# Conv mixer's LayerNorm in an encoder trunk: most statistics and flips ahead of the last tap group, smaller pieces after it, three weight subtractions on GpSimd

## The chip, the core and the metric

One of the eight cores of a Trainium2 chip runs the whole program; nothing is shared with the others. The metric is the device time of one execution in microseconds (us), lower is better; the median of three runs is given. A core has five engines with a queue each, and an engine takes its instructions strictly in the order in which they stand: TensorE (PE in the profile, PEld for its weight loads), VectorE (DVE), ScalarE (ACT), GpSimd (POOL) and SyncE (SP, which here only issues DMAs). They wait for each other on semaphores. Matmuls write to PSUM, in banks of 128 x 512 floats; all other tiles lie in SBUF.

## The reference, cut to what matters

The program computes four layers on 256 tokens of width 1024. Each layer has a token mixer (retention, convolution, attention, retention) and a SwiGLU FFN. Only the mixer of layer 1, the convolution, is touched:

```python
def _conv_mixer(h, w_in, b_in, w_dw, b_dw, ln_g, ln_b, w_out, b_out):
    a = h @ w_in + b_in
    u = a[..., :D_MODEL] * jax.nn.sigmoid(a[..., D_MODEL:])
    u = lax.conv_general_dilated(
        u, w_dw[:, None, :].astype(u.dtype), window_strides=(1,), padding=[(CONV_PAD, CONV_PAD)],
        dimension_numbers=('NWC', 'WIO', 'NWC'), feature_group_count=D_MODEL) + b_dw
    u = jax.nn.silu(_layernorm(u, ln_g, ln_b))
    return u @ w_out + b_out
...
x = x + _rmsnorm(m, norm_w[i, 1])
f = _swiglu(_rmsnorm(x, norm_w[i, 2]), ffn_w_in[i], ffn_w_out[i])
```

The depthwise convolution has 31 taps. The LayerNorm runs over all 1024 channels of a token, so its mean and variance need every channel of the convolution.

## The kernel before, in words

Matrix products keep nearly full float precision by splitting each operand x into a high part h, rounded to the type fp32r, and a low part l = x - h, and adding three matmuls (h h, h l, l h). `split` (L49) does this: ScalarE casts (L50), VectorE subtracts (L51). `load_w` (L62) loads 128 x 1024 weights by a DMA of SP into the tile `raw` (seven buffers) and splits them into `wh` and `wl`. The 256 tokens are two halves of 128, t = 0 and t = 1.

The convolution splits the channels. Channels 0 to 511 are done on VectorE with channels on the partitions (`taps`, L573): for each of four blocks `cb` one multiply and 30 multiply-adds `cv = upad * w + cv` (L577), then ScalarE adds the bias into `cvp` (L585). Channels 512 to 1023 are done on TensorE (`windows`, L592) with tokens on the partitions: each of two PSUM banks `pc` begins with two matmuls that put the bias in (L597) and gets four groups `q` of 16 matmuls (L604), 128 columns a group, 64 channels of both token halves.

The LayerNorm then needs tokens on the partitions. For each t, TensorE flips (transposes) the four blocks of `cvp` into the bank `bs` (L636); VectorE takes the statistics of 256 columns at a time, two from `bs` (L639) and two from the `pc` banks (L641), and joins them (L642); GpSimd makes 1/sqrt(variance + eps) as `rs` (`rsqrt_mean`, L112 and L113); VectorE computes -mean * rs (L644) and normalises the half from `bs` (L646, 512 columns), ScalarE the half from `pc` (L648, twice 256). The result `yc` is flipped back (L662), four blocks into one bank, and each block goes through `silu` with gain and bias on ScalarE (L665) into `sy`. A split of 512 columns at a time makes `yh`, `yl`, the stationary operands of the output projection (`out_block`, L200), 48 matmuls of 512 columns for each t.

The order of instructions on an engine isn't the text's alone: a scheduler at build time orders ready instructions by priority and its own idea of durations, and that order is fixed in the program. `tc.issue_after(i)` keeps an engine's instructions of the block behind `i` on that engine's queue. Here the three first tiles of `conv_w_out` (`CONV_EARLY`) have their split behind the last tap (`last_tap`), and the other five and the first FFN weights behind the split of t = 0's second half (`CONV_FENCE`, L677). After the projection, `finish` adds the residual, normalises, and the FFN starts with `flush(0)` (flips at L162) and matmuls at L183.

Of the kernel before, what the change touches and what calls it, by code (L numbers as in the profile page):

```python
# [8 lines left out]
F32 = mybir.dt.float32  # L9
F32R = mybir.dt.float32r  # L10
# [27 lines left out]
def tile_trunk(ctx: ExitStack, tc: tile.TileContext, a):  # L38
# [7 lines left out]
    def bank(tag):  # L46
        return ps.tile([P, 512], F32, tag=tag, name=tag, bufs=4 if tag == "acc" else 2)

    def split(h, l, src):  # L49
        ia = nc.scalar.copy(h, src)  # L50
        iv = nc.vector.tensor_sub(l, src, h.bitcast(F32))  # L51
        return ia, iv
# [9 lines left out]
    def load_w(src, cols=1024, pool=None, bufs=None):  # L62
# [8 lines left out]
        cast[0], cast[1] = split(h[:, :cols], l[:, :cols], raw[:, :cols])  # L71
        return h, l
# [441 lines left out]
    def conv(j, finish, pool, prefetch):  # L514
# [76 lines left out]

        def windows(bk):  # L592

            pc = bank("acc")
            sl = slice(bk * 512, bk * 512 + 512)
            for i, row in enumerate((brh, brl)):
                nc.tensor.matmul(pc, lhsT=ones.bitcast(F32R), rhs=row[:, sl], start=(i == 0), stop=False)  # L597
            for q in range(4):
                for hf in range(2):
                    tz = wp.tile([P, 1024], F32, tag="raw", name="raw", bufs=RAWBUFS)  # L600
                    nc.sync.dma_start(tz, a["conv_tz"][j, 4 * bk + q, hf])
                    for i in range(8):
# [6 lines left out]
                            stop=(q == 3 and d == SHIFTS - 1),  # L609
                        )  # L610
            return pc
# [11 lines left out]
        pcs = [windows(bk) for bk in range((KB - VB) // 2)]  # L623

        with tc.issue_after(last_tap["v"].ins):
            wo = [load_w(a["conv_w_out"][j, k]) for k in range(CONV_EARLY)]
# [4 lines left out]
        for t in range(2):  # L631
            bs = bank("mm")
            bn = work.tile([P, 4, 6], F32, tag="bn", name="bn", bufs=2)
            ms = work.tile([P, 8], F32, tag="lnm", name="lnm", bufs=2)
            for k in range(VB):
                nc.tensor.transpose(bs[:, k * P : (k + 1) * P], cvp[:, k, t * P : (t + 1) * P], ident)  # L636
            parts = [pc.rearrange("p (g t c) -> p g t c", t=2, c=64)[:, :, t, :] for pc in pcs]
            for hh in range(2):
                nc.vector.bn_stats(bn[:, hh, :], bs[:, hh * 256 : hh * 256 + 256])  # L639
            for hh in range(2):  # L640
                nc.vector.bn_stats(bn[:, 2 + hh, :], parts[hh])  # L641
            nc.vector.bn_aggr(ms[:, 0:2], bn)  # L642
# [3 lines left out]
            nc.vector.tensor_scalar(yc[:, 0:512], bs, ms[:, 0:1], rs, op0=ALU.subtract, op1=ALU.mult)  # L646
            for hh in range(2):
                nc.scalar.activation(  # L648
                    yc[:, 512 + 256 * hh : 768 + 256 * hh].rearrange("p (g c) -> p g c", c=64),
                    parts[hh],  # L650
                    AF.Identity,
                    scale=rs,
                    bias=ms[:, 2:3],
                )
            h = const.tile([P, KB, P], F32R, tag=f"xTh{t}", name=f"yh{t}")
            l = const.tile([P, KB, P], F32R, tag=f"xTl{t}", name=f"yl{t}")
            for hh in range(2):
# [5 lines left out]
                for k in range(4):  # L663
# [8 lines left out]
                ends = split(  # L672
                    h[:, 4 * hh : 4 * hh + 4, :].rearrange("p k t -> p (k t)"),
                    l[:, 4 * hh : 4 * hh + 4, :].rearrange("p k t -> p (k t)"),
                    sy.rearrange("p k t -> p (k t)"),
                )
# [348 lines left out]
```

## Time and profile before

| what | value |
|---|---|
| median of 3 runs (lowest to highest) | 1592.09 us (1591.9 to 1592.46) |
| the profiled execution | 1592.03 us, of which its span is 1590.3 us |
| DVE, ACT, POOL busy (share of the span) | 65%, 52%, 5% |
| first matmul of `windows` (L597) | 450.9 us |
| first matmul of the FFN after the convolution (L183) | 517.31 us |

Times in the profile run from the start of the span. A row of a timeline gives start, duration, engine, line, operation, tiles (out<-in) and the number of merged instructions; in square brackets stands how long the engine had been idle and what it had waited for. The table of windows gives for each stretch its length, then for each engine the busy time and count, then the TensorE clock that was granted (1.00 is full) and the DMA share.

### The profile page before, as it was taken

What the parts mean: (1) busy time and instruction counts of PE and PEld (TensorE: products, weight loads), DVE (VectorE), ACT (ScalarE), POOL (GpSimd) and SP (SyncE); (2) the same over time, 40 slices, a digit from 0 to 9 for tenths busy, and PEclk for the clock granted to TensorE, in tenths of its full rate; (3) what the DMA queues carried; (4) which work ended last, traced back from release to release, by engine and by line L of the source; (5) the groups of instructions that cost most, each with busy time, mean ns of one, the idle gap of its engine ahead of it and who ended that gap; (6) DMA issues with size and microseconds to landing.
All of it is one profiled execution on the core that took longest, in us unless ns stands there. A gap on an engine that the chain in (4) does not pass through costs nothing.

```text
span 1590.3 us, 21093 instructions
## 1 busy us (share of the span) xinstructions
PE 1565.7 (98%) x7792; PEld 1332.6 (84%) x7792; DVE 1036.6 (65%) x1575; ACT 834.2 (52%) x1291; POOL 83.3 (5%) x123
## 2 busy tenths in 40 slices
PE   9999999999998999999999999999999999999998
PEld 6888878888896888889999999788888888878886
DVE  7756685556698755558778777755468655675452
ACT  6544464445517644446666666644456444654441
POOL 1000010001111100010000000100011000100000
PEclk9999999999998999999999999999999999999999
DMA  8646466565456754534444444745555544475530
GB/s 312 230 141 198 138 232 213 171 209 175 154 164 230 262 201 159 189 126 151 152 149 150 130 136 159 262 167 206 186 185 176 183 164 134 157 238 201 183 119 27
DMA packets 82700, 283.19 MB, mean 178 GB/s; under 512 B 9890, under 2 KB 10146, under 8 KB 82596
## 3 DMA queue, kind: packets, MB, share of 16 engines
q1 hardware_dynamic: 82084, 281.32, 52.7%
q8 instruction: 61, 1.00, 0.2%
q0 software_dynamic: 512, 0.53, 0.1%
q14 instruction: 43, 0.35, 0.1%
HBM read 280.23 MB, written 1.05 MB: 177 GB/s over the span
## 4 chain that ended last, share of the span: by engine, by line
PE 87%; DVE 5%; ACT 3%; DMA 3%; issue 2%; POOL 0%; SPq 0%; DVEq 0%; POOLq 0%; ACTq 0%
PE mm L183 57%; PE acc L200 20%; DVE cv L577 2%; PE acc L804 1%; PE aux L459 1%; DMA raw<-in_ffn_w_out 1%; PE aux L324 1%; DVE wl L51 1%; ACT wh L50 1%; PE aux L789 1%; PE acc L763 1%; DMA raw<-in_ret_w_in 1%; PE acc L761 1%; PE aux L300 1%; PE aux L728 1%
## 5 line engine op out<-in xcount | busy, mean ns | idle before, releaser
L183 PE MATMUL mm<-wh,xTh 128*128 128x512 f32 (+1 forms) x1536 | 591.1, 385 | 1.1 <-ACT xTh L50 1.1
L183 PE MATMUL mm<-wl,xTh 128*128 128x512 f32 (+1 forms) x1536 | 579.7, 378 | 0.0
L183 PE MATMUL mm<-wh,xTl 128*128 128x512 f32 (+1 forms) x1536 | 579.2, 377 | 0.0
L51 DVE TENSOR_TENSOR wl<-raw,wh 128x1024 fp32r<-128x1024 f32 (+1 forms) x432 | 497.9, 1163 | 118.2 <-ACT wh L50 104.0
L50 ACT CAST wh<-raw 128x1024 fp32r<-128x1024 f32 (+1 forms) x432 | 429.8, 1004 | 159.6 <-PE mm L183 105.3
L183 PEld LDWEIGHTS mm<-wh,xTl 128*128 128x128 f32 x1536 | 288.7, 188 | 45.9 <-DVE xTl L51 0.3
L183 PEld LDWEIGHTS mm<-wh,xTh 128*128 128x128 f32 x1536 | 289.1, 188 | 43.5 <-ACT xTh L50 1.5
L183 PEld LDWEIGHTS mm<-wl,xTh 128*128 128x128 f32 x1536 | 289.5, 188 | 41.7 <-DVE wl L51 0.5
L448 ACT ACTIVATE fsg<-mm,rsx 128x256 f32<-128x256 f32 x88 | 41.7, 474 | 168.6 <-PE mm L183 168.5
L450 DVE SCALAR_TENSOR_TENSOR fsg<-mm,rsx,fsg 128x256 f32<-128x256 f32 x88 | 42.3, 481 | 124.8 <-ACT fsg L448 124.6
L51 DVE TENSOR_TENSOR pooll<-raw,poolh 128x1024 fp32r<-128x1024 f32 x88 | 107.2, 1222 | 6.9 <-ACT poolh L50 6.2
L200 PE MATMUL acc<-poolh,fhh 128*128 128x512 f32 x344 | 107.6, 393 | 0.5 <-ACT fhh L50 0.5
L200 PE MATMUL acc<-poolh,fhl 128*128 128x512 f32 x344 | 107.2, 392 | 0.0
L200 PE MATMUL acc<-pooll,fhh 128*128 128x512 f32 x344 | 106.1, 389 | 0.0
L50 ACT CAST poolh<-raw 128x1024 fp32r<-128x1024 f32 x88 | 92.7, 1054 | 23.4 <-PE acc L200 14.6
L51 DVE TENSOR_TENSOR fhl<-aux,fhh 128x256 fp32r<-128x256 f32 x88 | 37.0, 421 | 97.9 <-ACT fhh L50 97.9
L50 ACT CAST fhh<-aux 128x256 fp32r<-128x256 f32 x88 | 32.5, 369 | 116.3 <-PE aux L459 116.3
L200 PEld LDWEIGHTS acc<-poolh,fhh 128*128 128x128 f32 x344 | 63.7, 188 | 15.1 <-ACT fhh L50 2.7
L200 PEld LDWEIGHTS acc<-pooll,fhh 128*128 128x128 f32 x344 | 64.6, 188 | 13.5
L200 PEld LDWEIGHTS acc<-poolh,fhl 128*128 128x128 f32 x344 | 64.3, 188 | 13.5
L110 POOL TENSOR_SCALAR rs<-ss 128x1 f32<-128x1 f32 x16 | 7.2, 448 | 1034.3 <-ACT junk L118 1034.2
L577 DVE SCALAR_TENSOR_TENSOR cv<-upad,wdw,cv 128x256 f32<-128x256 f32 x120 | 49.0, 478 | 0.1
(186 smaller groups left out, 1573.9 us busy)
## 6 DMA issues: line engine op xcount, KB each, us to landing
raw<-in_ffn_w_in SPq DMA_DIRECT2D x176, 512.0 KB, 4.8
raw<-in_ret_w_in SPq DMA_DIRECT2D x96, 512.0 KB, 4.9
raw<-in_ffn_w_out SPq DMA_DIRECT2D x88, 512.0 KB, 4.6
raw<-in_attn_w_in SPq DMA_DIRECT2D x96, 384.0 KB, 3.6
raw<-in_ret_w_out SPq DMA_DIRECT2D x32, 512.0 KB, 4.4
raw<-in_conv_w_in SPq DMA_DIRECT2D x16, 512.0 KB, 5.0
raw<-in_conv_tz SPq DMA_DIRECT2D x16, 512.0 KB, 4.6
gain<-in_norm_w SPq DMA_DIRECT2D x15, 512.0 KB, 5.8
```

The source lines that it names most:

```text
L50: ia = nc.scalar.copy(h, src)
L51: iv = nc.vector.tensor_sub(l, src, h.bitcast(F32))
L183: nc.tensor.matmul(out, lhsT=st[t][:, k, :], rhs=mv[:, sl], start=(n == 0), stop=(n == 23))
L200: nc.tensor.matmul(acc[hh], lhsT=st, rhs=mv[:, hh * 512 : hh * 512 + 512], start=(first and i == 0), stop=(last and i == 2),)
L300: nc.tensor.matmul(b[:, m * 256 : (m + 1) * 256], lhsT=kt[:, 2 + half, m * P : (m + 1) * P], rhs=qt[:, half, :], start=(n == 0), stop=(n = ...
L324: nc.tensor.matmul(b, lhsT=pt[:, m, t * P : (t + 1) * P], rhs=vt[:, m, :], start=(n == 0), stop=(n == 5))
L448: nc.scalar.activation(sg, b[:, 0:256], AF.Silu, scale=rsx[t])
L450: nc.vector.scalar_tensor_tensor(out=sm, in0=b[:, 256:512], scalar=rsx[t], in1=sg, op0=ALU.mult, op1=ALU.mult)
L459: nc.tensor.transpose(tp[:, k * P : (k + 1) * P], sm[:, k * P : (k + 1) * P], ident)
L577: last_tap["v"] = nc.vector.scalar_tensor_tensor(out=cv, in0=upad[:, cb, w : w + 256], scalar=wdw[:, cb, w : w + 1], in1=cv, op0=ALU.mult, ...
L728: nc.tensor.transpose(tp[:, k * P : (k + 1) * P], rf[:, k * P : (k + 1) * P], ident)
L761: nc.tensor.matmul(b[:, 0:256], lhsT=x[:, 0, ts_(t)], rhs=y[:, h, :], start=(n == 0), stop=(n == 2))
```

## The change

Four things are edited, all for the end of the convolution's mixer.

1. `windows` is cut. Bank 0 is as before. In bank 1 the bias is put into the first three groups; behind group 2 stand the calls `early(0)` and `early(1)`, then the bias of the last 128 columns and group 3, the last tap group. `early(t)` flips blocks 0 to 2 of `cvp` into `bs[t]` and takes three statistics: bank 0 (256 columns), the three flipped blocks (384), and the first three groups of bank 1 (192).
2. Behind the last tap group remain for each t one flip (block 3), statistics of 128 and of 64 columns, and the joining of now five parts.
3. The normalisation is done in four quarters of 256 columns, by VectorE and ScalarE in turn, and the split behind the silu in pieces of two blocks (256 columns) instead of four.
4. The low parts of the three early tiles of `conv_w_out` are subtracted on GpSimd instead of VectorE (`sub=nc.gpsimd`).

```diff
-    def split(h, l, src):
+    def split(h, l, src, sub=None):
         ia = nc.scalar.copy(h, src)
-        iv = nc.vector.tensor_sub(l, src, h.bitcast(F32))
+        iv = (sub or nc.vector).tensor_sub(l, src, h.bitcast(F32))
         return ia, iv
...
+        def part(bk, t, lo, hi):
+            return pcs[bk].rearrange("p (g t c) -> p g t c", t=2, c=64)[:, lo:hi, t, :]
+
+        def early(t):
+            bs[t] = bank("mm")
+            for k in range(VB - 1):
+                nc.tensor.transpose(bs[t][:, k * P : (k + 1) * P], cvp[:, k, t * P : (t + 1) * P], ident)
+            nc.vector.bn_stats(bn[t][:, 0, :], part(0, t, 0, 4))
+            nc.vector.bn_stats(bn[t][:, 1, :], bs[t][:, 0 : 3 * P])
+            nc.vector.bn_stats(bn[t][:, 2, :], part(1, t, 0, 3))
...
+            cut = 3 if bk else 4
...
+            bias(0, cut)
             for q in range(4):
+                if q == cut:
+                    early(0)
+                    early(1)
+                    bias(cut, 4)
                 for hf in range(2):
...
-            wo = [load_w(a["conv_w_out"][j, k]) for k in range(CONV_EARLY)]
+            wo = [load_w(a["conv_w_out"][j, k], sub=nc.gpsimd) for k in range(CONV_EARLY)]
...
+            nc.tensor.transpose(bs[t][:, 3 * P : 4 * P], cvp[:, 3, t * P : (t + 1) * P], ident)
+            ms = work.tile([P, 16], F32, tag="lnm", name="lnm", bufs=2)
+            nc.vector.bn_stats(bn[t][:, 3, :], bs[t][:, 3 * P : 4 * P])
+            nc.vector.bn_stats(bn[t][:, 4, :], part(1, t, 3, 4))
+            nc.vector.bn_aggr(ms[:, 0:2], bn[t][:, 0:5, :])
             rs = rsqrt_mean(ms[:, 1:2], None, LN_EPS, scale=1.0)
...
-            nc.vector.tensor_scalar(yc[:, 0:512], bs, ms[:, 0:1], rs, op0=ALU.subtract, op1=ALU.mult)
...
+            quarter = (bs[t][:, 0:256], bs[t][:, 256:512], part(0, t, 0, 4), part(1, t, 0, 4))
+            for q4, src in enumerate(quarter):
+                dst = yc[:, 256 * q4 : 256 * q4 + 256]
...
+                if q4 % 2 == 0:
+                    nc.vector.tensor_scalar(dst, src, ms[:, 0:1], rs, op0=ALU.subtract, op1=ALU.mult)
+                else:
+                    nc.scalar.activation(dst, src, AF.Identity, scale=rs, bias=ms[:, 2:3])
...
-                ends = split(
-                    h[:, 4 * hh : 4 * hh + 4, :].rearrange("p k t -> p (k t)"),
...
+                    if k % 2:
+                        ends = split(
+                            h[:, cb - 1 : cb + 1, :].rearrange("p k t -> p (k t)"),
```

What the scheduler makes of it is seen in the order of the built programs. First TensorE's queue before, at the end of bank 1's last two pieces (L604 are the tap matmuls, L636 the flips of `cvp`, L662 the first flip of the normalised `yc`):

```order
L604 MATMUL acc<-raw,uw 128x128 [waits DMAHW2_49,DMASW7_49]
L604 MATMUL acc<-raw,uw 128x128 x7
L604 MATMUL acc<-raw,uw 128x128 [waits DMAHW3_49]
L604 MATMUL acc<-raw,uw 128x128 x7
L636 MATMUL mm<-ident,cvp 128x128 [waits Activation_49] x4
L636 MATMUL mm<-ident,cvp 128x128 x4
L662 MATMUL aux<-ident,yc 128x128 [waits DVE_49]
```

The same place of TensorE's queue now (L601 are the flips of `early`, L663 the two flips of block 3, L615 the bias, L634 the tap matmuls, L687 the flip of `yc`):

```order
L601 MATMUL mm<-ident,cvp 128x128 [waits Activation_49] x3
L601 MATMUL mm<-ident,cvp 128x128 x3
L663 MATMUL mm<-ident,cvp 128x128 [waits Activation_49]
L663 MATMUL mm<-ident,cvp 128x128 [waits DVE_49]
L615 MATMUL acc<-cbrh,ones 128x128 [waits DVE_49]
L615 MATMUL acc<-cbrl,ones 128x128
L634 MATMUL acc<-raw,uw 128x128 [waits DMAHW2_49,DMASW7_49]
L634 MATMUL acc<-raw,uw 128x128 x7
L634 MATMUL acc<-raw,uw 128x128 [waits DMAHW3_49]
L634 MATMUL acc<-raw,uw 128x128 x7
L687 MATMUL aux<-ident,yc 128x128 [waits DVE_49]
```

All eight flips, those of block 3 too, now stand ahead of the last tap group. The first L663 waits for ScalarE's `cvp` of block 3, made from the last tap; the second for VectorE's L603 of t = 1; and the bias L615 for VectorE's L604 of t = 1, which reads the same PSUM bank.

VectorE's queue before, from the last taps to the normalisation of t = 0 (L641 and L639 are statistics of `pc` and of `bs`):

```order
L577 SCALAR_TENSOR_TENSOR cv<-upad,wdw,cv 128x256 [waits DVE_49] x54
L641 BN_STATS bn<-acc 128x6 [waits PE_49]
L577 SCALAR_TENSOR_TENSOR cv<-upad,wdw,cv 128x256 [waits DVE_49] x3
L51 TENSOR_TENSOR wl<-raw,wh 128x1024 [waits DMAHW4_49,Activation_49]
L51 TENSOR_TENSOR wl<-raw,wh 128x1024 [waits DMAHW5_49,Activation_49]
L51 TENSOR_TENSOR wl<-raw,wh 128x1024 [waits DMAHW6_49,Activation_49]
L639 BN_STATS bn<-mm 128x6 [waits PE_49]
L639 BN_STATS bn<-mm 128x6
L641 BN_STATS bn<-acc 128x6
L639 BN_STATS bn<-mm 128x6 [waits PE_49]
L642 BN_AGGR lnm<-bn 128x2 [waits DVE_49]
```

VectorE's queue now at that place (L602, L603 and L604 are the statistics of `early`, first of t = 0, then of t = 1; L665 those of block 3, L666 those of the last tap group):

```order
L577 SCALAR_TENSOR_TENSOR cv<-upad,wdw,cv 128x256 [waits DVE_49] x54
L602 BN_STATS bn<-acc 128x6 [waits PE_49]
L577 SCALAR_TENSOR_TENSOR cv<-upad,wdw,cv 128x256 [waits DVE_49]
L603 BN_STATS bn<-mm 128x6 [waits PE_49]
L577 SCALAR_TENSOR_TENSOR cv<-upad,wdw,cv 128x256 [waits DVE_49]
L604 BN_STATS bn<-acc 128x6
L577 SCALAR_TENSOR_TENSOR cv<-upad,wdw,cv 128x256 [waits DVE_49]
L602 BN_STATS bn<-acc 128x6
L603 BN_STATS bn<-mm 128x6 [waits PE_49]
L604 BN_STATS bn<-acc 128x6
L665 BN_STATS bn<-mm 128x6 [waits PE_49] x2
L666 BN_STATS bn<-acc 128x6 [waits PE_49]
```

The three subtractions are gone from it, two more statistics stand between the last three taps, and those of t = 1 right behind them.

GpSimd's queue now, from the last of the DMAs that fill `uw` on (before, the three L51 rows weren't there, and nothing else differs):

```order
L566 DMA uw<-su 64x128 [waits DMASW7_49]
L51 TENSOR_TENSOR wl<-raw,wh 128x1024 [waits DMAHW4_49,PE_49,Activation_49]
L51 TENSOR_TENSOR wl<-raw,wh 128x1024 [waits DMAHW5_49,PE_49,Activation_49]
L51 TENSOR_TENSOR wl<-raw,wh 128x1024 [waits DMAHW6_49,PE_49,Activation_49]
L112 TENSOR_SCALAR rs<-lnm 128x1 [waits DVE_49]
L113 TENSOR_TENSOR rs<-rs,nhalf 128x1 [waits Pool_49]
```

The subtractions come ahead of the `rs` of both token halves. SP's queue has the same loads in the same order; three loads of `conv_w_out` that waited for VectorE's or TensorE's release of a `raw` buffer now wait for GpSimd's.

More of the change, by code (lines that the diff above doesn't have):

```diff
@@ L60, in tile_trunk, with load_w @@
     cast = [None, None]
[L62 removed]
+    def load_w(src, cols=1024, pool=None, bufs=None, sub=None):
         raw = wp.tile([P, 1024], F32, tag="raw", name="raw", bufs=RAWBUFS)
@@ L70, in load_w @@
             l = pool.tile([P, 1024], F32R, tag="pooll", name="pooll", bufs=bufs)
-        cast[0], cast[1] = split(h[:, :cols], l[:, :cols], raw[:, :cols])
+        cast[0], cast[1] = split(h[:, :cols], l[:, :cols], raw[:, :cols], sub)
         return h, l
@@ L590, in taps, with bias @@
             )
+        bs = [None, None]
+        bn = [work.tile([P, 8, 6], F32, tag="bn", name="bn", bufs=2) for t in range(2)]
+        def part(bk, t, lo, hi):
[7 more added lines that the diff above has]
+            nc.vector.bn_stats(bn[t][:, 2, :], part(1, t, 0, 3))
         def windows(bk):
             pc = bank("acc")
-            sl = slice(bk * 512, bk * 512 + 512)
-            for i, row in enumerate((brh, brl)):
-                nc.tensor.matmul(pc, lhsT=ones.bitcast(F32R), rhs=row[:, sl], start=(i == 0), stop=False)
+            pcs.append(pc)
+            cut = 3 if bk else 4
+            def bias(lo, hi):
+                for i, row in enumerate((brh, brl)):
+                    nc.tensor.matmul(
+                        pc[:, lo * P : hi * P],
+                        lhsT=ones.bitcast(F32R),
+                        rhs=row[:, bk * 512 + lo * P : bk * 512 + hi * P],
+                        start=(i == 0),
+                        stop=False,
+                    )
+            bias(0, cut)
             for q in range(4):
+                if q == cut:
+                    early(0)
+                    early(1)
+                    bias(cut, 4)
                 for hf in range(2):
@@ L608, in windows @@
                             start=False,
-                            stop=(q == 3 and d == SHIFTS - 1),
+                            stop=(q in (3, cut - 1) and d == SHIFTS - 1),
                         )
-            return pc
         wc = {}
@@ L622, in conv @@
             taps(cb)
-        pcs = [windows(bk) for bk in range((KB - VB) // 2)]
+        pcs = []
+        for bk in range(2):
+            windows(bk)
         with tc.issue_after(last_tap["v"].ins):
-            wo = [load_w(a["conv_w_out"][j, k]) for k in range(CONV_EARLY)]
+            wo = [load_w(a["conv_w_out"][j, k], sub=nc.gpsimd) for k in range(CONV_EARLY)]
         yh, yl = {}, {}
@@ L631, in conv @@
         for t in range(2):
[L632 to L642, printed above, removed]
+            nc.tensor.transpose(bs[t][:, 3 * P : 4 * P], cvp[:, 3, t * P : (t + 1) * P], ident)
[3 more added lines that the diff above has]
+            nc.vector.bn_aggr(ms[:, 0:2], bn[t][:, 0:5, :])
             rs = rsqrt_mean(ms[:, 1:2], None, LN_EPS, scale=1.0)
```

16 lines of the change are left out of this document (5 added, 11 removed).

## The prediction

> **What bounds the kernel now.** I read the page first, then the windows and waits around the end of the convolution, then the timelines of single engines there.
>
> ```profile
> span 1590.3 us, 21093 instructions
> PE 1565.7 (98%) x7792; PEld 1332.6 (84%) x7792; DVE 1036.6 (65%) x1575; ACT 834.2 (52%) x1291; POOL 83.3 (5%) x123
> PE 87%; DVE 5%; ACT 3%; DMA 3%; issue 2%; POOL 0%; SPq 0%; DVEq 0%; POOLq 0%; ACTq 0%
> ```
>
> TensorE sets the time; what is to be won are stretches where it waits or runs at a lower clock. The waits of TensorE between 474 and 520 us, and the windows (length, busy time and count of PE, PEld, DVE, ACT, POOL, then the granted clock, DMA share, GB/s):
>
> ```profile
> PE aux L662 <- DVE yc L646: 4.3, 1, 4.3
> PE aux L662 <- ACT sy L665: 1.2, 1, 1.2
> PE acc L200 <- DVE yl L51: 0.3, 1, 0.3
> 478.03:484.55 6.52, 4.51 (x41) 4.27 (x39) 6.45 (x12) 3.56 (x6) 0.00 (x0) 1.00 0.88 278
> 484.55:494.79 10.24, 6.82 (x23) 5.57 (x24) 6.41 (x14) 7.84 (x16) 1.49 (x4) 0.50 0.46 180
> ```
>
> The largest wait of this stage is 4.3 us for the normalised `yc`, and the clock is 0.50 for 10.24 us from 484.55 on. The timeline of TensorE, then of VectorE and ScalarE, shows what the wait consists of:
>
> ```profile
> 467.11 14.56 PE L604 MATMUL acc<-raw,uw 128*128 128x128 f32 x128
> ...
> 481.51 1.04 PE L636 MATMUL mm<-ident,cvp 128*128 128x128 f32 x8
> 486.81 1.97 PE L662 MATMUL aux<-ident,yc 128*128 128x128 f32 x8 [4.27 <-DVE yc L646]
> 489.94 1.09 PE L662 MATMUL aux<-ident,yc 128*128 128x128 f32 x4 [1.16 <-ACT sy L665]
> 490.68 1.20 PE L200 MATMUL acc<-wh,yh 128*128 128x512 f32 x2
> ```
>
> ```profile
> 475.74 2.45 DVE L577 SCALAR_TENSOR_TENSOR cv<-upad,wdw,cv 128x256 f32<-128x256 f32 x6
> 478.11 0.42 DVE L641 BATCH_NORM_STATS2 bn<-acc 128x6 f32<-128x256 f32 x1
> 478.45 1.50 DVE L577 SCALAR_TENSOR_TENSOR cv<-upad,wdw,cv 128x256 f32<-128x256 f32 x3
> 479.87 3.49 DVE L51 TENSOR_TENSOR wl<-raw,wh 128x1024 fp32r<-128x1024 f32 x3
> 483.28 0.75 DVE L639 BATCH_NORM_STATS2 bn<-mm 128x6 f32<-128x256 f32 x2
> 483.95 0.41 DVE L641 BATCH_NORM_STATS2 bn<-acc 128x6 f32<-128x256 f32 x1
> 484.28 0.41 DVE L639 BATCH_NORM_STATS2 bn<-mm 128x6 f32<-128x256 f32 x1
> 484.61 0.24 DVE L642 BATCH_NORM_AGGREGATE lnm<-bn 128x2 f32<-128x24 f32 x1
> 484.78 0.37 DVE L639 BATCH_NORM_STATS2 bn<-mm 128x6 f32<-128x256 f32 x1
> ...
> 485.95 0.80 DVE L646 TENSOR_SCALAR yc<-mm,lnm,rs 128x512 f32<-128x512 f32 x1
> ```
>
> ```profile
> 475.47 1.05 ACT L50 CAST wh<-raw 128x1024 fp32r<-128x1024 f32 x1 [19.27 <-DMA raw<-in_conv_w_out]
> ...
> 478.05 0.52 ACT L585 ACTIVATE cvp<-cv,chv 128x256 f32<-128x256 f32 x1
> 478.99 1.04 ACT L50 CAST wh<-raw 128x1024 fp32r<-128x1024 f32 x1 [0.42 <-DMA raw<-in_conv_w_out]
> 479.99 0.54 ACT L585 ACTIVATE cvp<-cv,chv 128x256 f32<-128x256 f32 x1
> ```
>
> The last tap group ends at 481.67 (467.11 + 14.56), the last tap at 479.95. Then VectorE does three subtractions (3.49 us) before its statistics, and TensorE waits. The change removes the 3.49 us from this chain. But before, the last tap group ran from 478.03 to 481.67 (a quarter of 14.56 is 3.64) beside the last taps; now, as the rows of TensorE's queue show, it stands behind flips and a bias that wait for the last tap and for statistics behind it. So the time of the last tap decides, and the three subtractions now run on GpSimd beside those taps.
>
> **The price of the subtractions on GpSimd.** No row shows one. The nearest rows (line, engine, operation, then busy time and mean ns of one; or start and duration):
>
> ```profile
> L532 POOL MEMSET uw<- 128x1152 f32 x1 | 1.1, 1063 | 5.3 <-PE acc L190 5.3
> L110 POOL TENSOR_SCALAR rsx<-ss 128x1 f32<-128x1 f32 x16 | 21.6, 1348 | 57.7 <-ACT junk L118 44.6 <-DVE xg L141 13.0
> 484.96 0.19 POOL L112 TENSOR_SCALAR rs<-lnm 128x1 f32<-128x1 f32 x1 [29.09 <-DVE lnm L642]
> 207.20 2.13 POOL L110 TENSOR_SCALAR rsx<-ss 128x1 f32<-128x1 f32 x1 [4.25 <-ACT junk L118]
> 206.81 2.35 DVE L51 TENSOR_TENSOR wl<-raw,wh 128x1024 fp32r<-128x1024 f32 x2
> 1399.76 0.82 POOL L110 TENSOR_SCALAR rsx<-ss 128x1 f32<-128x1 f32 x1 [2.46 <-ACT junk L118]
> 1399.80 1.29 DVE L141 TENSOR_TENSOR xg<-x,gain 128x512 f32<-128x512 f32 x2
> ```
>
> A memset writes 1152 columns in 1.063 us, so 1024 take 0.94: the lower end, one pass. Two inputs and an output one after the other are three passes, 2.83: the upper end. I take two passes, 1.9 us (two inputs in turn, the output beside).
>
> The other rows show a collision. A one-column operation of GpSimd takes 0.19 us while VectorE works from PSUM (484.96, beside the statistic at 484.78), but 2.13 us when it starts under two `wl` subtractions of VectorE, which read two SBUF tiles: it ends at 209.33, right behind them (209.16). The one at 1399.76 ended at 1400.58, half a us before the second of two `xg` products did (1401.09). So GpSimd is shut out while VectorE reads two SBUF tiles, and gets in after one or two of its instructions. A tap (`upad`, `cv`) is of that kind; a statistic from PSUM isn't. No row shows the reverse, a tap held up by a long GpSimd instruction, since none is long. Lower end: taps aren't held. Upper end: a tap waits for the whole subtraction. I take the upper end, since the row at 207.20 is such a full exclusion, seen from the other side.
>
> [...]
>
> **The sum.** It is made against the profiled execution, 1592.03 us (span 1590.3 and 1.73 around it), which is the median, 1592.09, to 0.06.
>
> 1. *Last tap.* Two statistics of 256 columns are 0.335 apart each (483.28 to 483.95), so the added ones, 384 and 192 columns, cost 0.50 and 0.25: 479.95 becomes 480.7. The first cast ends at 476.52, so GpSimd gets in at about 477.3, after one or two more taps of 0.4 us; the second and third follow with a tap or two between, all before the last tap (the third cast is late by then, behind the held `cvp` of block 2, and ends at about 481.2, before GpSimd asks for it). 3 x 1.9 = 5.7, of which some 0.6 hides under the PSUM statistics: **485.8**.
> 2. *Last tap group.* Statistics of t = 1 behind the tap, 0.34 + 0.50 + 0.25 = 1.1: the bias starts at 486.95 (`cvp` of block 3 and its two flips are done by then). Bias and group are 0.25 + 3.64 at full clock. TensorE will have been idle from 478.03 on but for eight flips (1.04), longer than the 4.27 that came with the clock of 0.50; there, half clock lasted 4.1 us into steady work (490.68 to 494.79). So 4.1 us do 2.05, 1.84 remain: end at **492.9** instead of 481.67.
> 3. *Group to `yc`.* Only 64 columns remain: 0.3 with the handshakes, then as before 484.61 to 485.95, 1.34: `yc` starts at 494.55, not 485.95. What remains of GpSimd's queue is long done.
> 4. *`yc` to the projection.* Before 485.95 to 490.68, 4.73. The pieces:
>
> ```profile
> 486.13 1.02 ACT L648 ACTIVATE yc<-acc,lnm,rs 128x256 f32<-128x256 f32 x2 [4.09 <-DVE lnm L644]
> 487.97 1.85 ACT L665 ACTIVATE sy<-aux,chv 128x128 f32<-128x128 f32 x5 [0.81 <-PE aux L662]
> 489.69 0.64 ACT L50 CAST yh<-sy 128x512 fp32r<-128x512 f32 x1
> ```
>
> ScalarE's pair starts 0.18 behind and takes 1.02; two flips 0.4; in ScalarE's queue three silus of 0.35 stand ahead of the first cast, half as wide, 0.4: 3.05, with a handshake 3.1. Gain 1.6. The projection starts at 494.55 + 3.1 = **497.65**, 7.0 later than 490.68.
> 5. *Behind it.* The idle stretch before the projection is again long, so half clock costs t = 0 what it did: 0. ScalarE's casts of the other five `conv_w_out` tiles start 3.0 instead of 1.5 after the projection's start (five silus, four pieces); they were needed with spare time:
>
> ```profile
> 492.19 6.78 ACT L50 CAST wh<-raw 128x1024 fp32r<-128x1024 f32 x7
> 493.32 5.77 DVE L51 TENSOR_TENSOR wl<-raw,wh 128x1024 fp32r<-128x1024 f32 x5 [0.25 <-ACT wh L50]
> 497.50 0.62 PE L200 MATMUL acc<-wl,yh 128*128 128x512 f32 x2
> ```
>
> The first `wl` of these is done at 494.55 and used at 497.50: of 2.95 spare, 1.4 remain. Without that cover it would cost up to 1.5. The loads that now wait for GpSimd's release of `raw` land well before these casts. For t = 1 the 0.3 wait for `yl` goes, and the queue has the flips of the next stage later; I count -0.5. From there on TensorE is full as before, so nothing is made good.
>
> Total: 7.0 - 0.5 = **+6.5 us, 1598.5**. With one pass for a subtraction (0.94) the three cost 2.9 less: +3.6; with three passes +9.3.
>
> **Rivals.**
>
> *The taps aren't held up (or GpSimd gives way).* The last tap ends at 480.9 (0.2 for the first flips, which need `cvp` of block 2 at 478.57), the bias starts at 482.0, the group ends at 485.9 at full clock or some 487.2 at half, `yc` starts 1.65 later, the projection 3.1 after that: 490.65 or 491.95, that is 0 or +1.3; with -0.5, **1591.5 to 1592.8**. For it: no row shows a held tap. If GpSimd comes only behind the taps, it ends at 480.9 + 5.7 = 486.6, about when `rs` is needed; at 2.83 us each `rs` would be 2.5 late, 1595.
>
> *Not slower: the clock doesn't fall at all.* The place is TensorE between 478.03 and the projection. If taps aren't held and the eight flips split the idle stretches so that the clock stays at 1.00, the group ends at 485.9, the projection starts as before, and it also saves what half clock cost from 490.68 to 494.79, half of 4.1: -2.05 - 0.5, **1589.5**. It decides when no idle piece is much longer than about 2 us (before, the clock fell 2.0 us after the flips of 481.51 to 482.55). Against it: flips at 479 and 480.5 leave some 3 of 4 us idle, and it needs the first rival too. Even so it is within 0.2%.
>
> *The statistics don't come early.* In part this is so whatever happens: the queue puts block 3's flips and the t = 1 statistics ahead of the last tap group. That is in all the sums.
>
> **How the numbers follow.** The forecast, tap and subtraction exclude each other, has 0.62; the first rival 0.23; the second 0.10; a subtraction above 2.83 us or a third stretch of half clock, above 1601.5, has 0.05. 0.2% is 3.2 us, about what a measurement of this kernel can tell from no change. Slower by more: nearly all of the forecast, the last case and a little of the first rival, 0.66. Within: 0.29, the rivals and the forecast's lowest end. Faster by more: 0.05, if the second saves more than I see. The likeliest case alone spans 1595.6 to 1601.3; for 8 in 10 the first rival is taken in: 1591.6 to 1601.8.
>
> **What would show it.** GpSimd's L51 at about 477.3, 480 and 482, each 1.9 us, with taps (L577) that start only when one ends: right; taps 0.4 apart throughout: wrong, the first rival. The last tap near 485.8; the bias L615 right behind the last L604; the tap group partly at clock 0.50; the wait of L687 short, some 2 us, and the projection near 497.65. If the projection starts before 492, the exclusion was wrong; if it starts late while the last tap is at 481, the clock or GpSimd's queue was the cause.

## The result and the profile after

| | before | after |
|---|---|---|
| median of 6 runs each (lowest to highest) | 1592.3 us (1591.9 to 1593.02) | 1601.31 us (1599.02 to 1602.14) |
| ratio, after to before | | 1.0056 (95% interval 1.0046 to 1.0066) |
| profiled execution, and its span | 1592.03 us, 1590.3 us | 1602.14 us, 1600.4 us |

The kernel became slower by 9 us. 1598.5 was predicted: the direction, the mechanism and the range (to 1601.8) held, the size was 2.8 us short, at the very end of what the likeliest case allowed (1601.3).

In the profiled execution after, the convolution was already reached some 1 us late: the first matmul of `windows` started at 451.85, before at 450.87. Nothing of the change lies ahead of it, and in a second profile of the same kernel (the last experiment) it started at 450.85. So times are compared from that matmul on, 0.98 being taken off what this profile shows.

TensorE's timeline after (start, duration, engine, line, operation, tiles, count, and in brackets the idle time and what ended it), from that first matmul to the projection:

```profile
451.85 0.49 PE L615 MATMUL acc<-cbrh,ones 1*128 1x512 f32 x1
...
467.97 10.98 PE L634 MATMUL acc<-raw,uw 128*128 128x128 f32 x96
478.79 0.38 PE L601 MATMUL mm<-ident,cvp 128*128 128x128 f32 x2
479.69 0.66 PE L601 MATMUL mm<-ident,cvp 128*128 128x128 f32 x4 [0.52 <-ACT cvp L585]
487.23 0.73 PE L663 MATMUL mm<-ident,cvp 128*128 128x128 f32 x2 [6.88 <-ACT cvp L585]
487.88 0.47 PE L615 MATMUL acc<-cbrh,ones 1*128 1x128 f32 x1
...
488.50 5.64 PE L634 MATMUL acc<-raw,uw 128*128 128x128 f32 x32
496.42 1.42 PE L687 MATMUL aux<-ident,yc 128*128 128x128 f32 x8 [2.28 <-DVE yc L677]
499.05 1.17 PE L200 MATMUL acc<-wh,yh 128*128 128x512 f32 x2 [1.21 <-ACT yh L50]
```

The wait for `yc` shrank from 4.27 to 2.28 us, as the change's smaller remainder of statistics would have it. But a new wait of 6.88 us for block 3's `cvp` stands ahead of the last tap group, which started at 488.50 (before, its quarter of the merged row began at 478.03). VectorE's timeline shows why `cvp` came late, and GpSimd's row who did it:

```profile
479.07 0.43 DVE L602 BATCH_NORM_STATS2 bn<-acc 128x6 f32<-128x256 f32 x1
479.41 2.25 DVE L577 SCALAR_TENSOR_TENSOR cv<-upad,wdw,cv 128x256 f32<-128x256 f32 x1
481.58 0.55 DVE L603 BATCH_NORM_STATS2 bn<-mm 128x6 f32<-128x384 f32 x1
482.06 2.08 DVE L577 SCALAR_TENSOR_TENSOR cv<-upad,wdw,cv 128x256 f32<-128x256 f32 x1
484.06 0.35 DVE L604 BATCH_NORM_STATS2 bn<-acc 128x6 f32<-128x192 f32 x1
484.34 2.28 DVE L577 SCALAR_TENSOR_TENSOR cv<-upad,wdw,cv 128x256 f32<-128x256 f32 x1
...
487.35 0.34 DVE L604 BATCH_NORM_STATS2 bn<-acc 128x6 f32<-128x192 f32 x1
...
494.18 0.23 DVE L666 BATCH_NORM_STATS2 bn<-acc 128x6 f32<-128x64 f32 x1 [5.89 <-PE acc L634]
...
495.83 0.54 DVE L677 TENSOR_SCALAR yc<-mm,lnm,rs 128x256 f32<-128x256 f32 x1
```

```profile
478.03 8.31 POOL L51 TENSOR_TENSOR wl<-raw,wh 128x1024 fp32r<-128x1024 f32 x3 [21.19 <-ACT wh L50]
```

A tap takes 0.4 to 0.5 us when nothing is in its way; the last three took 2.25, 2.08 and 2.28. In between, the statistics, which read PSUM, ran at their usual length (0.43, 0.55 and 0.35; with the subtractions on VectorE 0.43, 0.57 and 0.36). GpSimd's row of three subtractions spans 478.03 to 486.34, and the last tap ended at 486.62. That the one held the other is so far read from their lying side by side; the experiments test it.

The windows (length, busy time and count of PE, PEld, DVE, ACT, POOL, then granted clock, DMA share, GB/s) show where the clock was halved:

```profile
478.66:482.07 3.41, 1.17 (x9) 0.69 (x7) 3.41 (x6) 2.02 (x3) 3.41 (x2) 1.00 0.08 32
482.07:492.31 10.24, 5.08 (x22) 4.67 (x23) 6.17 (x9) 2.01 (x3) 4.27 (x2) 0.50 0.69 256
...
499.13:502.55 3.42, 3.42 (x9) 2.69 (x10) 1.81 (x5) 3.42 (x10) 0.00 (x0) 0.50 0.00 0
1024.79:1028.20 3.41, 3.41 (x12) 2.72 (x11) 2.10 (x5) 1.58 (x3) 0.00 (x0) 0.50 1.03 414
```

The last tap group ran at half clock until 492.31, the first 3.4 us of the projection did, and so did a stretch 500 us later, at the start of the FFN behind the attention, where before had full clock throughout.

### The profile page after: what moved, and what is told of

Read it like the earlier page. It is cut to its first block, busy times and chain, and to the rows that moved or that the text cites. A ratio compares the mean times of both kernels' runs of the same rounds, so it can differ in the third digit from the quotient of the medians.

```text
span 1600.4 us, 21109 instructions
## 1 busy us (share of the span) xinstructions
PE 1570.0 (98%) x7794; PEld 1335.6 (83%) x7794; DVE 1039.5 (65%) x1580; ACT 833.6 (52%) x1295; POOL 88.4 (6%) x126
## 4 chain that ended last, share of the span: by engine, by line
PE 89%; DVE 4%; ACT 3%; issue 1%; DMA 1%; POOL 1%; SPq 0%; DVEq 0%; POOLq 0%; ACTq 0%
PE mm L183 57%; PE acc L200 22%; DVE cv L577 2%; PE acc L830 1%; PE aux L459 1%; PE aux L324 1%; ACT wh L50 1%; PE aux L815 1%; DMA raw<-in_ffn_w_out 1%; PE acc L789 1%; PE aux L162 1%; PE acc L787 1%; PE aux L300 1%; PE aux L754 1%; DMA raw<-in_ret_w_in 1%
## 5 line engine op out<-in xcount | busy, mean ns | idle before, releaser
L51 DVE TENSOR_TENSOR wl<-raw,wh 128x1024 fp32r<-128x1024 f32 (+1 forms) x429 | 494.6, 1163 | 118.9 <-ACT wh L50 104.6
L51 DVE TENSOR_TENSOR pooll<-raw,poolh 128x1024 fp32r<-128x1024 f32 x88 | 107.3, 1222 | 7.7 <-ACT poolh L50 7.3
L51 DVE TENSOR_TENSOR fhl<-aux,fhh 128x256 fp32r<-128x256 f32 x88 | 37.1, 421 | 99.2 <-ACT fhh L50 99.2
L577 DVE SCALAR_TENSOR_TENSOR cv<-upad,wdw,cv 128x256 f32<-128x256 f32 x120 | 54.2, 526 | 0.1
```

Of the source, the lines that this page charges most:

```text
L51: iv = (sub or nc.vector).tensor_sub(l, src, h.bitcast(F32))
L577: last_tap["v"] = nc.vector.scalar_tensor_tensor(out=cv, in0=upad[:, cb, w : w + 256], scalar=wdw[:, cb, w : w + 1], in1=cv, op0=ALU.mult, ...
```

## The experiments

All numbers of place in this table are differences to the profile before, taken from each execution's own first matmul of `windows`: the end of the last tap (before 29.08 us behind it), the start of the projection (39.81), and the first flip in the attention of the next layer (265.91). The places come from the one execution of each kernel that was profiled. The times are medians of 5 to 11 executions (the run of the three forms: one), beside those of the kernel before on the same chip. The ratios aren't taken from the medians and can differ a little from their quotient.

| run | last tap | projection | attention | median, us | before, us | ratio (95%) |
|---|---|---|---|---|---|---|
| the change | +5.7 | +7.4 | +7.9 | 1601.31 | 1592.3 | 1.0056 (1.0046 to 1.0066) |
| change, subtractions on VectorE | +0.7 | +1.8 | +2.1 | 1594.88 | 1592.49 | 1.0017 (1.0008 to 1.0025) |
| before, subtractions on GpSimd | +5.7 | +3.4 | +3.7 | 1595.4 | 1592.49 | 1.0023 (1.0014 to 1.0032) |
| before, smaller pieces | 0.0 | -1.2 | +0.1 | 1591.49 | 1592.49 | 0.9996 (0.9987 to 1.0005) |
| before, pieces, subtractions behind `yc` | 0.0 | -3.0 | -1.6 | 1593.01 | 1592.49 | 1.0004 (0.9995 to 1.0013) |
| change, last tap group ahead | +5.7 | +3.7 | +4.2 | 1593.31 | 1592.27 | 1.0008 (0.9999 to 1.0017) |
| change, three forms on GpSimd | +2.1 | +4.0 | +4.5 | 1596.58 | 1592.27 | one run |
| pieces, statistics, then subtractions | 0.0 | -2.6 | -1.4 | 1591.94 | 1592.27 | 0.9997 (0.9989 to 1.0006) |
| the same with filler flips | 0.0 | -2.8 | -2.0 | 1588.77 | 1592.27 | 0.9979 (0.9970 to 0.9989) |
| the same, own columns | 0.0 | -2.8 | -3.6 | 1588.49 | 1591.39 | 0.9983 (0.9974 to 0.9992) |
| change repaired, with filler | +0.5 | -2.1 | -1.3 | 1590.12 | 1591.39 | 0.9998 (0.9988 to 1.0007) |
| before, filler alone | 0.0 | -0.8 | -2.7 | 1589.89 | 1591.39 | 0.9986 (0.9977 to 0.9995) |
| the change again | +5.7 | +7.5 | +8.0 | 1600.2 | 1591.16 | 1.0053 (1.0039 to 1.0067) |

### The changed kernel with the subtractions back on VectorE

```diff
-            wo = [load_w(a["conv_w_out"][j, k], sub=nc.gpsimd) for k in range(CONV_EARLY)]
+            wo = [load_w(a["conv_w_out"][j, k]) for k in range(CONV_EARLY)]
```

> The changed kernel with the three early subtractions back on VectorE, where they stand behind the statistics of t = 1 and ahead of those of block 3; TensorE's order is as after the change. If GpSimd's subtractions hold the taps, no tap takes over 0.6 us now, the last tap ends at about 480.9 instead of 486.6, the last tap group at 486 to 487, the projection starts at 490.7 to 492, and the time is 1592 to 1594.5. If the place of the last tap group behind flips and statistics is the cost, wherever the subtractions run, the projection still starts after 496 and the time stays above 1598.

VectorE's timeline of it, the last tap and the subtractions, then TensorE's:

```profile
480.67 0.47 DVE L577 SCALAR_TENSOR_TENSOR cv<-upad,wdw,cv 128x256 f32<-128x256 f32 x1
...
482.12 3.48 DVE L51 TENSOR_TENSOR wl<-raw,wh 128x1024 fp32r<-128x1024 f32 x3
```

```profile
482.73 5.32 PE L634 MATMUL acc<-raw,uw 128*128 128x128 f32 x32
...
492.98 1.22 PE L200 MATMUL acc<-wh,yh 128*128 128x512 f32 x2 [1.22 <-ACT yh L50]
```

The last tap takes 0.47 again, and the 3.48 us of subtractions now lie under the last tap group. Of the change's 7.4 us at the projection 1.8 are left, and of its 9 us in the medians 2.4. So GpSimd's share, with TensorE's order untouched, is 5.6 us at the projection. (The median is 0.4 us above the range expected.) The rival that the order alone is the cost (projection after 496) falls; but the order isn't free either: although fewer statistics and smaller pieces stand behind the group, the projection still starts 1.8 us later than before.

### The kernel before with the subtractions on GpSimd

```diff
-            wo = [load_w(a["conv_w_out"][j, k]) for k in range(CONV_EARLY)]
+            wo = [load_w(a["conv_w_out"][j, k], sub=nc.gpsimd) for k in range(CONV_EARLY)]
```

> The kernel before with one part of the change, the three early subtractions on GpSimd. If GpSimd gets in only where VectorE reads from PSUM, there is one such place here (the statistic at 478.1): one tap is held for about 2.2 us, the last tap ends at 481.7, the other two subtractions run beside statistics until about 486, rs comes some 1 us late, and the time is about 1593 (1592 to 1594). If GpSimd gets in behind any tap, three taps are held, the last tap ends at about 485.5, and the time is 1595.5 to 1597, since the flips and statistics follow. If nothing is held, the 3.49 us go from VectorE and the time falls to about 1589.

VectorE's row of the last three taps, and GpSimd's of the subtractions:

```profile
478.60 7.22 DVE L577 SCALAR_TENSOR_TENSOR cv<-upad,wdw,cv 128x256 f32<-128x256 f32 x3
```

```profile
476.98 8.56 POOL L51 TENSOR_TENSOR wl<-raw,wh 128x1024 fp32r<-128x1024 f32 x3 [20.95 <-ACT wh L50]
```

Three taps in a row without a statistic between them took 7.22 us, 2.4 each: the second guess was right, not the one that I had put first. GpSimd was ready at 476.98, while taps went on 0.4 us apart, and held none until the statistic at 478.26 (VectorE's only work from PSUM there); from then on a subtraction and a tap took turns. Here the tap group runs beside the held taps, and the price is 3.4 us at the projection, not 7.4. It is less than the 5.7 us of the last tap because VectorE, without its 3.49 us of subtractions, goes from the last tap (485.82) to `yc` (489.49) in 3.67 us; before it took 6.00.

### The changed kernel with the last tap group ahead

```diff
-            nc.vector.bn_stats(bn[t][:, 2, :], part(1, t, 0, 3))
...
-            nc.tensor.transpose(bs[t][:, 3 * P : 4 * P], cvp[:, 3, t * P : (t + 1) * P], ident)
+            with tc.issue_after(group["v"].ins):
+                nc.tensor.transpose(bs[t][:, 3 * P : 4 * P], cvp[:, 3, t * P : (t + 1) * P], ident)
...
-            nc.vector.bn_stats(bn[t][:, 4, :], part(1, t, 3, 4))
+            nc.vector.bn_stats(bn[t][:, 2, :], part(1, t, 0, 4))
```

`group["v"]` is the last matmul of the last tap group.

> The changed kernel, subtractions still on GpSimd, but the last tap group no longer behind the last tap: the early statistic of bank 1's first three groups is left out (256 columns are taken behind the group instead of 64) and block 3's flips stand behind the group. By my theory three taps are still held (last tap at about 485.5), but the group runs beside them and ends at about 484; the projection starts at about 491.5 instead of 499, and the time is 1594 to 1596.5, near that of the kernel before with the subtractions on GpSimd (1595.4). If the place of the group is not what multiplies the hold, the projection still starts after 496 and the time is above 1599.

TensorE's timeline of it:

```profile
481.90 6.36 PE L634 MATMUL acc<-raw,uw 128*128 128x128 f32 x32
488.11 0.38 PE L664 MATMUL mm<-ident,cvp 128*128 128x128 f32 x2
...
493.87 1.22 PE L200 MATMUL acc<-wh,yh 128*128 128x512 f32 x2 [0.90 <-ACT yh L50]
```

The last tap is as late as in the change (+5.7), yet the projection is late by 3.7 instead of 7.4, and the median by 1.0 instead of 9.0. The group ended later than I expected (488.26 instead of 484; the flips ahead of it waited 2.6 us for `cvp` of block 2, which was held up too, and it ran at half clock), but beside the held taps and not behind them. The median, 1593.31, even lies below the range expected: five of the ten executions took 1591.8 to 1592.31 us, the other five 1594.3 to 1596.3, and the profiled one, 1596.03, is among the long ones, so its places overstate what is left in the median. So the two edits cost more together than one by one: held taps cost 3.4 to 3.7 us at the projection where the group runs beside them, the order costs 1.8 where the taps aren't held, and both together 7.4, since each held tap then also holds TensorE. (The runs aren't alike in all else, the smaller pieces for one, so this is no exact sum.)

### Other work in GpSimd's three places

```diff
-            wo = [load_w(a["conv_w_out"][j, k], sub=nc.gpsimd) for k in range(CONV_EARLY)]
+            wo = [load_w(a["conv_w_out"][j, k], sub=(lambda l, s: nc.gpsimd.memset(l.bitcast(F32), 0.0), lambda l, s: nc.gpsimd.tensor_copy(l, s), lambda l, s: nc.gpsimd.tensor_sub(l, s, s))[k]) for k in range(CONV_EARLY)]
```

> The changed kernel with other work in GpSimd's three places: a memset of wl (writes only), a copy raw to wl (one input), and raw - raw (two reads); the low parts of these three weights are so left out or wrong in value, and the time stands for itself alone. If only reads of two inputs shut VectorE out, the taps run 0.4 us apart beside the memset and the copy, and one tap takes over 2 us beside the last. If any access of GpSimd does, a tap takes about 1 us beside the memset too. If a copy holds as well, two taps are held, by about 1 and 2.2 us.

GpSimd's timeline, then VectorE's at the same times:

```profile
433.02 0.98 POOL L657 MEMSET wl<- 128x1024 f32 x1
...
477.98 2.16 POOL L657 CAST wl<-raw 128x1024 fp32r<-128x1024 f32 x1 [21.05 <-DMA raw<-in_conv_w_out]
480.12 2.05 POOL L657 TENSOR_TENSOR wl<-raw 128x1024 fp32r<-128x1024 f32 x1
```

```profile
431.53 2.35 DVE L51 TENSOR_TENSOR wl<-raw,wh 128x1024 fp32r<-128x1024 f32 x2
...
479.16 0.43 DVE L602 BATCH_NORM_STATS2 bn<-acc 128x6 f32<-128x256 f32 x1
479.50 0.92 DVE L577 SCALAR_TENSOR_TENSOR cv<-upad,wdw,cv 128x256 f32<-128x256 f32 x1
480.34 0.55 DVE L603 BATCH_NORM_STATS2 bn<-mm 128x6 f32<-128x384 f32 x1
480.82 1.63 DVE L577 SCALAR_TENSOR_TENSOR cv<-upad,wdw,cv 128x256 f32<-128x256 f32 x1
```

The memset went earlier, since it waits for no load, but beside VectorE's subtractions of two SBUF tiles: it took 0.98 us (the nearest such row before: 1152 columns in 1.06), and VectorE's two took 2.35, as at the same place before (2.35 at 430.47). So in this one place writing alone doesn't collide. The copy, with one input, was queued at 477.98, got in at the statistic of 479.16 and held the next tap (0.92). The subtraction of `raw` from itself held one for 1.63. In these rows it is the forms that read that collide, and the price goes with how long GpSimd's row lasts once it is in: some 1.0 us for 1024 elements of one input (479.16 to 480.14), 2.05 with two reads.

### The smaller pieces alone, and the subtractions somewhere else on VectorE

The first run takes only the quarters and the split of 256 columns into the kernel before.

> The kernel before with one part of the change, the normalisation in quarters and the split behind the silu in pieces of 256 columns. By my sum the projection starts 1.6 us sooner (489.1 instead of 490.68) and the time is 1590 to 1591. If the pieces cost as much in more instructions and in later casts of the other conv_w_out tiles as they give, the time stays at 1592 or is up to 1 us above.

The projection came 1.2 us sooner, near the sum's 1.6, but at the attention nothing was left, and the medians can't be told apart. TensorE's timeline at the FFN's start, of before, then with the pieces:

```profile
514.14 1.26 PE L162 MATMUL aux<-ident,xg 128*128 128x128 f32 x8 [0.43 <-DVE xg L141]
515.16 0.47 PE L200 MATMUL acc<-wl,yh 128*128 128x512 f32 x1
515.47 0.62 PE L200 MATMUL acc<-wh,yl 128*128 128x512 f32 x2
515.93 0.62 PE L200 MATMUL acc<-wh,yh 128*128 128x512 f32 x2
...
517.31 0.39 PE L183 MATMUL mm<-wh,xTh 128*128 128x512 f32 x1
```

```profile
515.89 1.26 PE L162 MATMUL aux<-ident,xg 128*128 128x128 f32 x8 [0.55 <-DVE xg L141]
516.90 0.47 PE L200 MATMUL acc<-wh,yl 128*128 128x512 f32 x1
517.28 0.50 PE L183 MATMUL mm<-wh,xTh 128*128 128x512 f32 x1
...
518.82 0.50 PE L183 MATMUL mm<-wh,xTl 128*128 128x512 f32 x1 [0.34 <-DVE xTl L51]
```

Before, nine matmuls of the projection of t = 1 stood between the flips of `xg` and the FFN and covered the making of `xTh` and `xTl` (2.15 us from 515.16 to 517.31). With the pieces the scheduler leaves one, and TensorE waits for `xTl`. That wait of 0.3 us is in the profile of every kernel with the pieces except the one with the subtractions right behind `yc`, and in none without them.

The second run also puts the three subtractions behind the normalisation of t = 0:

```diff
-        with tc.issue_after(last_tap["v"].ins):
-            wo = [load_w(a["conv_w_out"][j, k]) for k in range(CONV_EARLY)]
...
+            if t == 0:
+                with tc.issue_after(yi.ins):
+                    wo = [load_w(a["conv_w_out"][j, k]) for k in range(CONV_EARLY)]
```

> The kernel before with the pieces of the change, and with the three early subtractions on VectorE but behind the normalisation of t = 0 instead of ahead of the statistics. The statistics then start when the flips are done: yc starts at about 484.2 instead of 485.95, the projection at about 487.4 instead of 490.68, and the time is 1588 to 1589.5. If the subtractions in their new place make the low parts of yh or of the first weights late, it is as the run with the pieces alone, 1590 to 1591.5.

`yc` started at 484.15 and the projection at 487.38, both as expected, but the time didn't follow. VectorE's timeline shows the first leak:

```profile
491.14 8.00 DVE L51 TENSOR_TENSOR wl<-raw,wh 128x1024 fp32r<-128x1024 f32 x7
499.06 0.21 DVE L642 TENSOR_SCALAR lnm<-lnm,rs 128x1 f32<-128x1 f32 x1
499.18 0.54 DVE L650 TENSOR_SCALAR yc<-mm,lnm,rs 128x256 f32<-128x256 f32 x1
```

The normalisation of t = 1 fell behind seven further subtractions, and the projection of t = 1 waited 1.21 us for `yh`. The next run mends that: statistics of both halves first, two subtractions behind `yc` of t = 0 and the third behind the first piece of `yl`. (In that run and in the first one with the filler, t = 0's half of `yc` from the `pc` banks is normalised from the columns of t = 1; the instructions and sizes are the same.)

> The kernel before with the pieces, the three subtractions on VectorE behind the normalisation of t = 0, and the statistics of t = 1 ahead of them. In the run with the subtractions behind yc the normalisation of t = 1 stood behind ten subtractions (yc of t = 1 at 499.2) and the projection of t = 1 waited 1.21 us for yh. That wait should go: the projection of t = 0 at 487.4, the first FFN matmul 3 us sooner than before (514.3 instead of 517.3), and the time 1588 to 1590. If ScalarE's seven casts ahead of t = 1 are what made it late, the wait stays and the time is 1591 to 1593.

That wait went, and the FFN began sooner (514.91), but the median stayed within 0.3 us of before. The windows of this run name a second leak:

```profile
485.00:491.82 6.82, 5.92 (x18) 4.37 (x18) 6.50 (x12) 6.00 (x15) 0.32 (x1) 0.50 0.60 190
1014.06:1017.48 3.42, 3.42 (x12) 2.83 (x11) 1.93 (x4) 1.78 (x4) 0.00 (x0) 0.50 0.96 376
```

TensorE is busy in 5.92 of 6.82 us at the convolution's end, at half clock, and in the whole of a stretch at 1014 us. The lead of 1.4 us at the attention turned into a lag of 0.8 us behind that stretch.

### Filler for the clock

```diff
+                if t == 0 and hh == 0:
+                    with tc.issue_after(fl.ins):
+                        for k in range(16):
+                            nc.tensor.transpose(tp[:, (k % 4) * P : (k % 4 + 1) * P], ident, ident)
```

`fl` is the last flip of `cvp` ahead of it; the flips of `yc` then overwrite `tp`.

> As the run with the statistics ahead of the subtractions, with 16 flips of a constant on TensorE (results unused) between the flips of cvp and those of yc, to see what the half clock costs. If the clock falls because TensorE stood still, one or two of the half-clock stretches of 3.41 us go and the time is 1 to 3 us lower (1586 to 1589). If the flips themselves run at half clock or last longer than the wait for yc, the projection is late by the excess, up to 1.5 us, and nothing is won.

> As the run with the filler flips, but with the normalisation of t = 0 reading its own columns of the pc banks (there and in the run without the filler it read those of t = 1, in the same sizes). Nothing else changes, so the time is again 1587 to 1590, some 3 us below the kernel before, if the gain was the filler's and no chance of that chip's runs. If it was chance, it is 1591 to 1593 as without the filler.

> The kernel before with nothing but 28 flips of a constant (results unused) on TensorE in the wait of 4.27 us for yc. If half clock at the start of the projection costs what the trace shows (4.1 us at 0.50, so 2.05, and the yc flips at half clock some 0.5), and standing still causes it, the time falls by 1.5 to 2.5 us to 1590 to 1591 and the yc flips run at full clock. If the clock falls all the same, or the flips delay those of yc, it stays at 1592 or is above.

With the filler the median fell from 1591.94 to 1588.77 on one chip, and with t = 0's own columns it is 1588.49 on another; the filler alone in the kernel before gives 1589.89 beside 1591.39. (There it is 28 flips, and the scheduler put t = 1's flips of `cvp` behind those of `yc`.) The windows of the run with its own columns, then of the filler alone:

```profile
487.44:500.00 12.56, 12.56 (x58) 10.03 (x59) 12.21 (x17) 12.26 (x23) 0.00 (x0) 1.00 0.85 288
```

```profile
481.70:500.00 18.30, 14.84 (x90) 12.47 (x90) 15.12 (x24) 14.13 (x26) 1.49 (x4) 1.00 0.62 218
```

In these two profiles the clock stayed at 1.00 where before had 10.24 us at 0.50. In the first run with the filler one stretch of 3.41 us was left (488.56 to 491.97), where the run without it had 6.82. Filling the wait thus kept the clock up in whole or in part, so standing still is what halves it there. What that costs is less sure. The filler alone took 1.5 us off the median. Of the 3.2 us of the first run with it, its profile has only 0.6 at the attention (-2.0 against -1.4); most of the rest comes behind it, where the run without the filler has the stretch of 3.42 us at 1014.06 and this one none. The run with the filler and its own columns beats both kernels: 0.9983 of before (0.9974 to 0.9992).

### The change repaired

All of the change's early flips and most of its early statistics, but the last tap group ahead of block 3's flips, the subtractions behind `yc`, and the filler.

> The idea of the change without its two faults: early flips and early statistics of bank 0 and of the flipped blocks, the last tap group ahead of block 3's flips, the three subtractions on VectorE behind yc of t = 0, the pieces, and the filler. The early flips stand ahead of the last tap group and put its end from 481.7 to about 482.6; behind it one statistic more than without them. By my reading early statistics are worth nothing here, since the statistics were done as soon as the flips were: yc starts some 0.9 us later than in the run without them, and the time is 1 us above it, 1588.5 to 1591. If early statistics pay, it is 1 us or more below it.

The projection started 0.8 us later than in that best run (-2.1 against -2.8), and the median is 1.6 us above it (1590.12 and 1588.49). The sign is as expected. Its profile also has one half-clock stretch that the other lacks, so how much of the 1.6 us is the early work's is not settled; that early statistics pay is not borne out.

### The change once more

> The changed kernel once more, for the part of the miss that lies outside the convolution. In its first profiled execution the FFN after the convolution began 7.6 us later than before, measured from the same place of the program's start (8.59 less 0.97), and some 2 us more came at 1015 to 1028 us, at the next place where TensorE waits, with a half-clock stretch of 3.41 us. If that stretch is chance (where the clock's grid falls), this execution shows again 7.4 to 8 us at the FFN's start, the 2 us may be missing, and the times spread from 1599 to 1602. If it belongs to the change, it is there again and no time is below 1600.5.

Started at the same place as before (450.85), this execution shows the steps without an offset: last tap at 485.61, projection at 498.19, attention 8.0 us late. The stretch at half clock was there again:

```profile
1024.08:1027.49 3.41, 3.41 (x12) 2.73 (x11) 2.08 (x4) 1.36 (x3) 0.00 (x0) 0.50 1.00 401
```

Yet three of the five times lay below 1600.5 (1598.15 to 1601.04), so neither guess is borne out whole: the stretch is more than a rare chance, and the times still spread by 3 us. The 7.6 us that the expectation names for the FFN's start doesn't stand in the first profile: its first matmul there started at 525.37, which is 7.1 us late behind `windows`, and here it is 7.2.

## Why the prediction was right, and where it was short

The mechanism was the one forecast (0.62 of the chance): taps and GpSimd's subtractions exclude each other, and the last tap group stands behind the last tap.

1. *Last tap*: 485.8 predicted; 486.62, less the offset 0.98, is 485.64, and 485.61 in the second profile. Two errors cancelled. A subtraction holds longer than 1.9 us: the three held taps lost 1.8, 1.6 and 1.8 us against a normal 0.47, with some 0.3 to 0.5 more hidden under each statistic, so about 2.1. And together they hide more under the statistics than the 0.6 us that I had counted, some 1.3 (three times 2.1, less the 5.0 by which the last tap is later than in the run with the subtractions on VectorE). How GpSimd gets in was put wrongly: not after one or two taps, but at a statistic that reads PSUM, in all five profiles with reads on GpSimd there, 1.0 to 1.6 us after its record begins.
2. *Last tap group*: bias at 486.95 and end at 492.9 predicted; 486.90 and 493.16. The half clock came as forecast, until 492.31.
3. *Group to `yc`*: 494.55 predicted, 494.85 measured.
4. *`yc` to the projection*: 3.1 predicted, 3.22 measured; the projection 7.0 later predicted, 7.4 measured.
5. *Behind it*: this is the step that failed. I had -0.5; up to the FFN's first matmul it was -0.3 (7.1 of the 7.4 were left), as the shorter half clock and the missing wait for `yl` would have it. Then the FFN's start cost 0.8, for the flips of the next stage, which I counted as a gain, moved past the matmuls that had covered `xTh` and `xTl`. That is 1 us of the miss. TensorE's wait there in the change:

```profile
526.92 0.50 PE L183 MATMUL mm<-wh,xTl 128*128 128x512 f32 x1 [0.33 <-DVE xTl L51]
```

The other 2 us of it in the profiled executions came where the sum had nothing, at 1015 to 1028 us: TensorE waits there for `fsg` in both kernels (1.55 us before, 1.92 after), and after it the clock was halved for 3.41 us. "From there on TensorE is full as before" was not so: a third stretch had 0.05 of the chance. From 1592.03 to 1602.14: 0.98 of a later start, 7.4 at the projection, 0.5 from there to the attention, 2.0 at 1015 to 1028, less 0.7 at the end of the program. The later start isn't in the second profile, so that part of the profiled difference isn't the change's.

The rivals: that the taps aren't held is ruled out by the held taps themselves and by the run with the subtractions on VectorE. That the clock doesn't fall needed the first, so it never came up in the change; the price it named, 2 us, is near what the filler won in the kernel before (1.5 us in the medians, 2.2 by the ratio).

The far stretch at half clock is in six profiles (the change twice, and four of the variants) and not in the other eight, and the profiles show what goes with it. Within one execution such stretches begin at whole multiples of 3.413 us from each other: in the change at 482.07 and 1024.79, which is 159 times, in the run with the statistics ahead of the subtractions at 485.00 and 1014.06, 155 times. With each execution cut into pieces on its own such grid, TensorE was by its records busy for 0.35 to 0.45 of the piece ahead of the stretch in the six profiles, and for 0.51 or more of every piece around the same wait in the other eight (in the change 1.49 of the 3.41 us from 1021.38 on; before 2.84 and 2.44 of the two pieces from 1010.20 on). So it also counts where the wait falls: a wait of 1.92 us inside one piece (the change, 0.44) was followed by half clock, while the longest, 2.36 us from 1017.04 to 1019.40 (the kernel before with the subtractions on GpSimd), is divided between two (0.70 and 0.60) and was not.

What stays open: the bound isn't that sharp at the convolution's end, where a piece of 0.56 was followed by half clock (the first run with the filler) and one of 0.45 was not (the filler alone). Nor does anything here say beforehand where the grid will fall: the change's first stretch began 30.22 us behind the first matmul of `windows` in one execution and 30.51 in the other.

## What to carry to other kernels

Work moved to an idle engine is not free where the two get in each other's way: GpSimd's three subtractions beside a VectorE chain of two SBUF inputs held that chain for 5.0 to 5.7 us, where VectorE itself does them in 3.5, while the statistics from PSUM beside them kept their length (0.43, 0.55 and 0.35 us), and a memset beside two of VectorE's own subtractions left those at 2.35 us. Before putting work ahead of a matmul group, look at what the built order makes that group wait for: the price of any delay upstream is then paid by TensorE as well. A gain at one wait is worth what is left at the next places where TensorE stands still, so measure it there too, and where TensorE must wait some microseconds, a filler can be worth more than a shorter wait: here it took 1.5 us off the kernel before, while the three runs that brought the projection forward without it can't be told apart from that kernel.

## What was not expected of the hardware

GpSimd did not get in between taps that follow each other 0.4 us apart (it waited from 476.98 to 478.3 beside three of them), and took turns with them once it was in (7.22 us for three taps). Why it got in at the statistic and then between taps too isn't shown.

All stretches at half clock from the convolution to the far one last multiples of 3.41 us (3.41, 6.82, 10.24, once 13.65), and they begin at other places of the program in each run. A wait of 1.92 us was followed by one (1024.79), a wait of 1.55 us at the same place of the program before was not. One stretch of 3.41 us with TensorE busy throughout is worth about 1.7 us, an estimate from its half clock. The kernel before spread from 1590.26 to 1595.02 us over 32 runs of one chip; how much of that comes from such stretches isn't shown, since one of its executions is profiled.
